# Dilated attention with queries and keys put in class order, a ones column in V, copies on GpSimd and loads queued between the quads

## The chip, the cores and the metric

The kernel runs on one core of a Trainium2 chip. The metric is the device time of one execution in microseconds (us), from runs on the chip; the kernel before takes 2574.51 us (median of 3 runs, 2571.3 to 2576.02). One further execution was profiled. TensorE is called PE, VectorE DVE, ScalarE ACT and GpSimd POOL; SP is the engine whose queue issues the DMAs.

## The reference, cut to what matters

Two transformer blocks follow each other over 1024 tokens of width 1024, in fp32. The change is inside the attention of the second block (8 heads of width 64), which mixes three dilated windows. Each branch is a softmax over keys at a distance that is a multiple of its dilation, and the branches are joined by their softmax denominators:

```python
DILATED_BRANCHES = ((128, 1), (512, 4), (2048, 16))

def dilated_window_branch(q, k, v, rel_bias, window, dil):
    half = window // (2 * dil)          # query p attends to keys p + dil*j, |j| <= half
    ...
    s = jnp.einsum('brnqhd,brnkhd->brnhqk', qb, kw).astype(jnp.float32)
    s = s + bias.transpose(2, 0, 1)
    s = jnp.where(valid[:, None], s, NEG_INF)
    m = jnp.max(s, axis=-1, keepdims=True)
    p = jnp.exp(s - m)
    den = jnp.sum(p, axis=-1, keepdims=True)
    o = jnp.einsum('brnhqk,brnkhd->brnqhd', (p / den).astype(v.dtype), vw)
    lse = (m + jnp.log(den))[..., 0].transpose(0, 1, 2, 4, 3)
    ...
    return o, lse

def dilated_attention(q, k, v, rel_bias):
    outs, lses = [], []
    for window, dil in DILATED_BRANCHES:
        o, l = dilated_window_branch(q, k, v, rel_bias, window, dil)
        outs.append(o)
        lses.append(l)
    w = jax.nn.softmax(jnp.stack(lses, axis=0), axis=0)
    return jnp.einsum('ibsh,ibshd->bshd', w.astype(q.dtype), jnp.stack(outs, axis=0))
```

The mixture of softmaxes is one softmax over all the keys of the three branches, a key counted once for each branch that has it.

## The kernel before, in words

Nearly all of the time is matmuls of weights against activations, each as three products of split operands (a high and a low part). The dilated attention stands between the projection of q and k (`d_run("qk", ...)`, line 1564) and the output projection (`wp_group`), at about 1684 to 1860 us of the span.

It is cut into quads: one quad (`dil_quad`, line 1805) is 128 queries of four heads. Branches 4 and 16 only join positions of one residue modulo 4, so they are done together as *class quads*: class c holds the 256 positions c, c+4, c+8, ..., and its bias carries log 2 where both branches have a key. There are 16 of them: `u` (which four heads) by `qb` (first or second 128 queries of the class) by `c`. The branch of dilation 1 is done in 16 *band quads*: 128 queries in a row, against 256 keys in a row (192 at the two ends).

The steps of a quad are a Python generator; `pump` (line 232) starts one new quad and lets each older one make a step, the youngest first, so the steps of several quads are interleaved in program order on every engine, and each engine runs its own order without overtaking. The steps: (1) `scores` (line 1254) makes eight PE matmuls, four with the 128-row operands and four with the 64-row low parts; DVE adds the bias and finds the row's extreme (L1831); ACT takes the exponential and sums it (L1834). (2) PE transposes the probabilities (L1842), ACT and DVE copy them out (L1845, L1847). (3) PE multiplies with V (L1861) and DVE copies the result (L1863). A class quad then writes its rows, the extremes and the sums to a DRAM buffer `cls_d` (L1865). A band quad loads the class rows of its own queries (tile `xc`, L1822, issued in its first step), and merges both with small DVE operations (L1870 to L1876) and POOL multiplications (L1877 to L1881); (4) two more PE transposes (L1887) put the result in the layout of the output projection (L1889, L1890).

Queries (`query_operand`, tiles `qst`) and keys (`key_operand`, tiles `kst`) are stored in token order. A class quad therefore reads both with a step of four elements (`qc`, `kc` in `scores`). V is loaded from DRAM: `vc` by class, four DMAs of 512 KB; `vb` for the bands, nine DMAs of up to 256 KB (L1575), all of them ahead of the first class quad on SP. The bias comes by `bias_load` (tiles `cb` for classes, `bb` for bands).

Tiles named `S` share 43 slots of 4 KB; a new tile waits until its slot's last reader is done. The row buffer `co` of a class quad comes from a ring of six. DMAs take turns on eight semaphores, so each waits for the one eight places ahead of it on SP.

Some of the split of the next weights runs on POOL while the band quads run (`self.low = nc.gpsimd`, L281).

Of the kernel before, what the change touches and what calls it, by code (L numbers as in the profile page):

```python
# [175 lines left out]
class Kern:  # L176
# [1062 lines left out]
    def key_operand(self):  # L1239

        nc = self.nc
        k = [self.S("kst", dt=F32R) for _ in range(3)]
        def put(h, ps):
            sl = slice(512 * h, 512 * h + 512)
            for s in range(2):
                pr = slice(64 * s, 64 * s + 64)
                nc.scalar.copy(k[s][pr, sl], ps[pr, :])
            for s in range(2):
                pr, po = slice(64 * s, 64 * s + 64), slice(64 - 64 * s, 128 - 64 * s)
                nc.vector.tensor_tensor(k[2][pr, sl], ps[pr, :], k[s][pr, sl].bitcast(F32), ALU.subtract)  # L1250
                nc.scalar.copy(k[s][po, sl], ps[pr, :])
        return k, put

    def scores(self, sc, qs, ks, q0, k0, step, nk):


        nc = self.nc
        qc = slice(q0 % 512, q0 % 512 + step * (P - 1) + 1, step)
        kc = slice(k0, k0 + step * (nk - 1) + 1, step)
        th = q0 // 512  # L1260
        for j in range(2):
            for s in range(2):
                nc.tensor.matmul(sc[s][:, 256 * j : 256 * j + nk], qs[j][th][:, s, qc], ks[j][s][:, kc],
                                 start=(j == 0), stop=False, skip_group_check=True)
        for j in range(2):
            for s in range(2):
                pr = slice(64 * s, 64 * s + 64)
                nc.tensor.matmul(sc[s][:, 256 * j : 256 * j + nk], qs[j][th][pr, s, qc], ks[j][2][pr, kc],
                                 start=False, stop=(j == 1), skip_group_check=True)


    def att1_quad(self, n, u, aq, ak, av, att):
# [6 lines left out]
        self.scores(sc, aq[2 * u : 2 * u + 2], [ak, ak], n * P, k0, 1, nk)  # L1279
# [168 lines left out]
    def block2(self, Z, x2_d):  # L1448
# [75 lines left out]
        def vc_load(c):  # L1524
            t = self.S("vc", [P, 2, 512])
            nc.sync.dma_start(t, vsrc[c].rearrange("(b p) c -> p b c", p=P))
            vc.append(t)

        vc, cb = [], []
        cls_d = dp.tile([SEQ, 2, 264], F32, name="cls_d")  # L1530
        qs, ks, kput = [None] * 4, [None] * 4, [None] * 4
        qput = [None] * 4
        cls = [self.dil_quad("c", (c, qb), u, qs, ks, vc, cb, cls_d)
# [3 lines left out]
        def qk_evac(p, s, ps):  # L1537
# [8 lines left out]
            if ch == 0:  # L1546
                if p == 1:
                    qs[s], qput[s] = self.query_operand()
                qput[s](th, src)
            else:  # L1550
                if p == 3:
                    ks[s], kput[s] = self.key_operand()
                kput[s](th, src)
            if p == 7 and s == 0:
                vc_load(0)
                cb.extend(self.bias_load(0, 384, "cb", range(4)))
            if p == 4 and s == 0:
                for c in range(1, 4):
                    vc_load(c)
# [7 lines left out]
        cb += self.bias_load(0, 384, "cb", range(4, 8))  # L1567
# [4 lines left out]
        vb = [self.S("vb", [P, 2, 512]) for _ in range(5)]  # L1572
        for m in range(9):
            lo, hi = max(0, P * m - 64), min(SEQ, P * m + 64)
            nc.sync.dma_start(vb[m // 2][0 : hi - lo, m % 2, :], v_d[lo:hi, :])  # L1575
        bb = self.bias_load(L_CLS, 256, "bb")
        while self.pend:
            self.pump()
# [14 lines left out]

        lead = 13
        gpo = self.bcast("gpo", a["g_post_mix_2"][0])
        self.low = nc.gpsimd
        wl = None
        for u in range(2):
            for n in range(NT):
                self.pend.append(self.dil_quad("b", n, u, qs, ks, vb, bb, cls_d, MX))  # L1600
                self.pump()
                i = NT * u + n
# [202 lines left out]
    def dil_quad(self, kind, where, u, qs, ks, vt, bias, cls_d, MX=None):  # L1805

        nc = self.nc
        if kind == "c":
            c, qb = where
            q0, k0, step, nk, b0 = c + 512 * qb, c, 4, 256, 128 - 128 * qb  # L1810
            segs = [(0, P, vt[c][:, 0, :]), (P, P, vt[c][:, 1, :])]
            co = self.H("co", [P, 264])
        else:
            n = where
            lo, hi = max(0, P * n - 64), min(SEQ, P * n + 192)
            q0, k0, step, nk, b0 = n * P, lo, 1, hi - lo, lo - (P * n - 64)
            segs = []
            for m in (n, n + 1):
                a0, a1 = max(0, P * m - 64), min(SEQ, P * m + 64)
                segs.append((a0 - lo, a1 - a0, vt[m // 2][0 : a1 - a0, m % 2, :]))  # L1820
            x2 = self.S("xc", [P, 2, 264])
            nc.sync.dma_start(x2[:, 0, :], cls_d[n * P : n * P + P, u, :])  # L1822
            co = x2[:, 1, :]
        sc = [self.PS("sc") for _ in range(2)]
        self.scores(sc, qs[2 * u : 2 * u + 2], ks[2 * u : 2 * u + 2], q0, k0, step, nk)
        z = self.S("z", [P, 4, 256])
        for s in range(2):
            for j in range(2):
                h, x = 4 * u + 2 * j + s, 2 * j + s
                nmc = co[:, 256 + x : 257 + x]  # L1830
                nc.vector.tensor_tensor_reduce(  # L1831
                    out=z[:, x, :nk], in0=sc[s][:, 256 * j : 256 * j + nk], in1=bias[h][:, b0 : b0 + nk], scale=-0.125,
                    scalar=BIG, op0=ALU.add, op1=ALU.min, accum_out=nmc)
                nc.scalar.activation(z[:, x, :nk], z[:, x, :nk], AF.Exp, bias=nmc, scale=-1.0,  # L1834
                                     accum_out=co[:, 260 + x : 261 + x])
        yield
        pT = self.S("pT", [P, 8, P])
        for g in range(2):
# [4 lines left out]
            if kind == "c" or segs[0][1] == segs[1][1]:  # L1843
# [14 lines left out]
        for x in range(4):  # L1858
            h = 4 * u + x
# [64 lines left out]
```

## Time and profile before

| | |
|---|---|
| runs, median (lowest to highest) | 2574.51 us (2571.3 to 2576.02) |
| profiled execution, its own time | 2574.72 us |
| its span | 2572.9 us |
| PE busy | 2504.7 us (97%) |
| DVE, ACT, POOL busy | 1765.6, 1142.2, 178.7 us |
| mean granted TensorE clock | 0.988 |

The span runs from the first to the last instruction; the profiled execution's own time is 1.8 us longer and 0.2 us above the median. PE is counted busy from a matmul's start to its modelled end, and the matmuls are pipelined, so a 97% busy PE may still hold short gaps. What a stage costs is read from the chain of waits, which gives each stretch of time to the instruction that held the end up.

### The profile page before, as it was taken

The page shows a single profiled execution, that of the slowest core. Times are in us where ns is not written, and L with a number is a line of the kernel's source. Part 1 is how long each engine was busy: PE and PEld are TensorE (multiplying, and loading weights), DVE is VectorE, ACT ScalarE, POOL GpSimd, SP SyncE. Part 2 cuts the span into 40 slices and gives each one's busy share as a digit, 9 for nine tenths or more (in the row PEclk, how much of TensorE's full clock was granted, in tenths as well). Part 3 has the DMA queues.
Part 4 walks back from the last instruction along what each step waited for, and adds up shares of the span by engine and source line. Part 5 has one row for each costly group of instructions (what it writes and reads, how often), then busy time and mean ns, then how long its engine had stood idle before and what let it go on. Part 6 is the DMA issues. An engine that isn't in the chain of part 4 may idle for free.

```text
span 2572.9 us, 31324 instructions
## 1 busy us (share of the span) xinstructions
PE 2504.7 (97%) x11857; PEld 2073.0 (81%) x11857; DVE 1765.6 (69%) x2789; ACT 1142.2 (44%) x2068; POOL 178.7 (7%) x236
## 2 busy tenths in 40 slices
PE   7999999999999999999999999999999999899998
PEld 5888888888787888878788777888887888788886
DVE  7664456556899755555799986666558444478888
ACT  5444445412425433333333644566436555553334
POOL 1000000000002000000000300002421000000006
PEclk9999999999999999999999999999899999999999
DMA  4333333135343122233433415221242333522334
GB/s 157 104 110 103 123 103 107 39 113 185 109 186 131 66 70 87 87 130 98 174 121 131 144 49 172 102 81 51 81 160 82 104 117 103 180 108 81 115 123 147
DMA packets 178703, 291.57 MB, mean 113 GB/s; under 512 B 10168, under 2 KB 84552, under 8 KB 178552
## 3 DMA queue, kind: packets, MB, share of 16 engines
q1 hardware_dynamic: 178552, 289.57, 33.1%
q8 instruction: 93, 1.52, 0.2%
q14 instruction: 58, 0.48, 0.1%
HBM read 212.89 MB, written 80.31 MB: 114 GB/s over the span
## 4 chain that ended last, share of the span: by engine, by line
PE 78%; DVE 13%; DMA 3%; ACT 3%; issue 2%; POOL 1%; SPq 0%; DVEq 0%; ACTq 0%; POOLq 0%
PE da L1201 6%; PE a L500 6%; PE a L502 6%; PE a L501 6%; PE da L1200 6%; PE da L1199 6%; PE db L1201 3%; PE db L1200 3%; PE db L1199 3%; PE b L502 3%; PE b L501 3%; PE b L500 3%; DVE wl L281 3%; PE pv L1861 2%; DVE midl L281 2%
## 5 line engine op out<-in xcount | busy, mean ns | idle before, releaser
L500 PE MATMUL a<-midh,ws 128*128 128x512 f32 x708 | 276.8, 391 | 9.1 <-DVE f L1669 8.0
L502 PE MATMUL a<-midh,ws 128*128 128x512 f32 x708 | 276.4, 390 | 0.0
L501 PE MATMUL a<-midl,ws 128*128 128x512 f32 x708 | 276.4, 390 | 0.0
L1201 PE MATMUL da<-wh,midl 128*128 128x512 f32 x624 | 245.1, 393 | 6.6 <-DVE midl L281 6.6
L1200 PE MATMUL da<-wl,midh 128*128 128x512 f32 x624 | 244.6, 392 | 3.4 <-DVE wl L281 3.4
L1199 PE MATMUL da<-wh,midh 128*128 128x512 f32 x624 | 246.0, 394 | 0.6 <-ACT midh L279 0.6
L279 ACT CAST midh<-mt 128x1024 fp32r<-128x1024 f32 x80 | 82.9, 1036 | 244.6 <-DVE mt L1142 81.3
L1201 PE MATMUL db<-wh,midl 128*128 128x512 f32 x436 | 171.0, 392 | 3.5 <-DVE midl L281 3.5
L1200 PE MATMUL db<-wl,midh 128*128 128x512 f32 x436 | 170.8, 392 | 2.2 <-DVE wl L281 2.2
L1199 PE MATMUL db<-wh,midh 128*128 128x512 f32 x436 | 171.1, 392 | 1.4 <-ACT midh L279 1.4
L500 PEld LDWEIGHTS a<-midh,ws 128*128 128x128 f32 x708 | 133.4, 188 | 38.7 <-issue 8.9
L501 PEld LDWEIGHTS a<-midl,ws 128*128 128x128 f32 x708 | 133.5, 189 | 27.7
L502 PEld LDWEIGHTS a<-midh,ws 128*128 128x128 f32 x708 | 133.5, 189 | 27.7
L279 ACT CAST ws<-tc 128x512 fp32r<-128x512 f32 x180 | 111.4, 619 | 88.3 <-DVE tc L414 87.1
L1201 PEld LDWEIGHTS da<-wh,midl 128*128 128x128 f32 x624 | 117.8, 189 | 34.5 <-DVE midl L281 10.3
L1200 PEld LDWEIGHTS da<-wl,midh 128*128 128x128 f32 x624 | 117.9, 189 | 29.0 <-DVE wl L281 4.8
L500 PE MATMUL b<-midh,ws 128*128 128x512 f32 x360 | 140.1, 389 | 0.0
L501 PE MATMUL b<-midl,ws 128*128 128x512 f32 x360 | 140.1, 389 | 0.0
L502 PE MATMUL b<-midh,ws 128*128 128x512 f32 x360 | 140.0, 389 | 0.0
L279 ACT CAST wh<-raw 128x1024 fp32r<-128x1024 f32 x121 | 120.6, 1037 | 42.0 <-DMA raw<-in_w_ff_dram 15.2
L1199 PEld LDWEIGHTS da<-wh,midh 128*128 128x128 f32 x624 | 118.0, 189 | 26.0 <-issue 1.2
L281 DVE TENSOR_TENSOR wl<-raw,wh 128x1024 fp32r<-128x1024 f32 x117 | 136.2, 1197 | 3.6 <-ACT wh L279 3.5
(348 smaller groups left out, 5822.8 us busy)
## 6 DMA issues: line engine op xcount, KB each, us to landing
raw<-in_w_ff_dram SPq DMA_DIRECT2D x31, 1024.0 KB, 5.4
mid_d<-f SPq DMA_DIRECT2D x108, 256.0 KB, 2.1
midr<-mid_d SPq DMA_DIRECT2D x52, 512.0 KB, 6.9
raw<-in_w_in_dram SPq DMA_DIRECT2D x22, 1024.0 KB, 5.4
x<-x_d SPq DMA_DIRECT2D x24, 512.0 KB, 4.5
raw<-in_w_up_dram SPq DMA_DIRECT2D x11, 1024.0 KB, 5.6
raw<-in_w_gate_dram SPq DMA_DIRECT2D x10, 1024.0 KB, 5.5
xt<-in_x_dram SPq DMA_DIRECT2D x16, 512.0 KB, 10.9
```

What stands on the lines that cost most here:

```text
L279: self.nc.scalar.copy(hi, s)
L281: e.tensor_tensor(lo, s, hi.bitcast(F32), ALU.subtract)
L500: nc.tensor.matmul(ps, hi[:, i], xh, start=(first and i == 0), stop=False, skip_group_check=True)
L501: nc.tensor.matmul(ps, hi[:, i], xl, start=False, stop=False, skip_group_check=True)
L502: nc.tensor.matmul(ps, lo[:, i], xh, start=False, stop=(i == 3), skip_group_check=True)
L1199: nc.tensor.matmul(ps, xh, wh, start=(kt == 0 and p in (1, 5, 2)), stop=False, skip_group_check=True)
L1200: nc.tensor.matmul(ps, xh, wl, start=False, stop=False, skip_group_check=True)
L1201: nc.tensor.matmul(ps, xl, wh, start=False, stop=(kt == m - 1), skip_group_check=True)
L1861: nc.tensor.matmul(pv[:, 64 * x : 64 * x + 64], pT[0:w, 2 * x + e, :], vv[:, 64 * h : 64 * h + 64], start=(e == 0), stop=(e == 1))
```

## The change

In words, part by part:

- Keys are stored class after class (`key_operand(4)`): the ACT and DVE operations that write them read their source with a step of four.
- Queries get a second copy in class order (`q_class`, tiles `qc`): 16 copies of 128x512, four of them on ACT and 12 on POOL. Class quads read `qc` and the keys without a step; band quads read `qst` and 256 keys in runs of 32. The four band quads at the ends make 16 score matmuls in place of 8.
- V tiles have 65 columns per head, the 65th filled with ones by POOL, so the product with V also gives the sum of the exponentials. ACT no longer sums (L1834's accumulate goes). V for the bands is loaded class by class, by heads: 36 DMAs of 32 rows (or 16) by four runs of 256 B for each `u`, 72 in place of nine. The classes' V is 16 DMAs in place of four.
- A band quad starts its extreme from that of its class rows, so these must have landed before its first DVE step; they are loaded one quad ahead (`c_load`). The merge becomes one POOL multiplication of the class rows, one DVE addition, a reciprocal and one POOL multiplication. Band quads get an empty step after the first.
- A class quad's result is copied out of PSUM by ACT, no longer by DVE.
- The loads move on SP: biases for heads 4 to 7, V for `u = 1`, V for the bands and their biases now stand between the class quads, V for the second half of the bands after band quad 4. POOL puts the band biases into class order (8 copies of 128x256).

The diff, cut to its core:

```diff
-    def key_operand(self):
+    def key_operand(self, r=1):
...
+            w = 512 // r
+            v = [x.rearrange("p (r j) -> p r j", r=r)[:, :, w * h : w * h + w] for x in k]
+            ps = ps.rearrange("p (j r) -> p r j", r=r)
             for s in range(2):
                 pr = slice(64 * s, 64 * s + 64)
-                nc.scalar.copy(k[s][pr, sl], ps[pr, :])
+                nc.scalar.copy(v[s][pr], ps[pr])
...
-    def scores(self, sc, qs, ks, q0, k0, step, nk):
+    def scores(self, sc, qs, ks, q, keys):
...
-                nc.tensor.matmul(sc[s][:, 256 * j : 256 * j + nk], qs[j][th][:, s, qc], ks[j][s][:, kc],
-                                 start=(j == 0), stop=False, skip_group_check=True)
+                for i, (o, n, f) in enumerate(keys):
+                    nc.tensor.matmul(sc[s][:, 256 * j + o : 256 * j + o + n], q(qs[j])[:, s], f(ks[j][s]),
+                                     start=(j == i == 0), stop=False, skip_group_check=True)
...
+        def v_slot(name, vs, u, i):
+            if i % 3 == 0:
+                t = self.S(name, [P, 3, 260])
+                nc.gpsimd.memset(t.rearrange("p s (h d) -> p (s h) d", d=65)[:, :, 64:65], 1.0)
...
+        def vb_load(u, m):
+            lo, hi = max(0, 32 * m - 16), min(256, 32 * m + 16)
+            v, w = v_slot("vb", vb, u, m), hi - lo
+            for c in range(4):
+                nc.sync.dma_start(
+                    v[c * w : c * w + w], vsrc[c, lo:hi, 256 * u : 256 * u + 256].rearrange("p (h d) -> p h d", d=64))
+
+        def q_class(s, th, copy):
+            yield
+            qc[s][th] = t = self.S("qc", [P, 2, 512], F32R)
+            for i in range(2):
+                copy(t[:, i, :].rearrange("p (r j) -> p r j", r=4), qs[s][th][:, i, :].rearrange("p (j r) -> p r j", r=4))
...
+            if step in (2, 3):
+                self.pend.extendleft(q_class(x, step - 2, nc.gpsimd.tensor_copy) for x in (2, 3))
+                self.pump(2)
+            if step == 4:
+                cb += self.bias_load(0, 384, "cb", range(4, 8))
+            if step == 5:
+                for i in range(8):
+                    vc_load(1, i)
+            if step == 11:
+                for m in range(9):
+                    vb_load(0, m)
+            if step in (11, 12):
+                h = 4 * (step - 11)
+                b, t = self.bias_load(L_CLS, 256, "bn", range(h, h + 4)), self.S("bb", [P, 4, 256])
+                for i in range(4):
+                    nc.gpsimd.tensor_copy(t[:, i, :].rearrange("p (g r j) -> p g r j", g=2, r=4),
+                                          b[i].rearrange("p (g j r) -> p g r j", g=2, r=4))
...
+        wl, nxt = None, c_load(0)
...
+                i = NT * u + n
+                x2, nxt = nxt, c_load(i + 1) if i < 15 else None
+                self.pend.append(self.dil_quad("b", n, u, qs, ks, vb, bb, x2, MX))
                 self.pump()
+                if i == 4:
+                    for m in range(9):
+                        vb_load(1, m)
...
+                least = BIG if kind == "c" else x2[:, 0, 260 + x : 261 + x]
+                for o, w, fb, fz in parts:
+                    nc.vector.tensor_tensor_reduce(
+                        out=fz(z[:, x, o : o + w]), in0=fz(sc[s][:, 256 * j + o : 256 * j + o + w]), in1=fb(bias[h]),
+                        scale=-0.125, scalar=least, op0=ALU.add, op1=ALU.min, accum_out=nm)
+                    least = nm
+                nc.scalar.activation(z[:, x, :nk], z[:, x, :nk], AF.Exp, bias=nm, scale=-1.0)
+        if kind == "b":
+            d = self.M("d", 4)
+            nc.gpsimd.tensor_tensor(d, co[:, 260:264], x2[:, 0, 260:264], ALU.subtract)
+            nc.scalar.activation(d, d, AF.Exp)
+            v = x2[:, 0, 0:260].rearrange("p (h d) -> p h d", d=65)
+            nc.gpsimd.tensor_tensor(v, v, d[:, :, None].to_broadcast([P, 4, 65]), ALU.mult)
+            yield
         yield
...
-        nc.vector.tensor_tensor(mn, x2[:, 0, 256:260], x2[:, 1, 256:260], ALU.min)
-        nc.vector.tensor_tensor(d, mn[:, None, :].to_broadcast([P, 2, 4]), x2[:, :, 256:260], ALU.subtract)
-        nc.scalar.activation(e, d, AF.Exp)
-        yield
-        nc.vector.tensor_tensor(d, e, x2[:, :, 260:264], ALU.mult)
-        nc.vector.tensor_tensor(rc, d[:, 0, :], d[:, 1, :], ALU.add)
-        nc.vector.reciprocal(rc, rc)
...
+        nc.vector.tensor_tensor(co[:, 0:260], pv[:, 0:260], x2[:, 0, 0:260], ALU.add)
+        sums = co[:, 0:260].rearrange("p (h d) -> p h d", d=65)
+        rc = self.M("rc", 4)
+        nc.vector.reciprocal(rc, sums[:, :, 64])
+        y = x2[:, 0, 0:256]
+        nc.gpsimd.tensor_tensor(y.rearrange("p (h d) -> p h d", d=64), sums[:, :, 0:64],
+                                rc[:, :, None].to_broadcast([P, 4, 64]), ALU.mult)
```

Three places show how the order moves. The first is SP's queue around the V of the bands, where `vb` is that V, `bn`/`bb` the band biases, `cls_d` the class quads' rows and `co` the row buffer of one class quad. Before:

```order
L1444 DMA cb_13182<-bias_d_8839 128x2x384
L1575 DMA vb_13184<-v_d 64x512
L1575 DMA vb_13184<-v_d 128x512
L1575 DMA vb_13185<-v_d 128x512 x2
L1575 DMA vb_13186<-v_d 128x512 x2
L1575 DMA vb_13187<-v_d 128x512 x2
L1575 DMA vb_13188<-v_d 64x512
L1444 DMA bb_13198<-bias_d_8839 128x4x256
L1444 DMA bb_13200<-bias_d_8839 128x4x256
L1865 DMA cls_d<-co_13160 128x264
L1865 DMA cls_d<-co_13202 128x264
```

With the change, the same engine at the rows of class quads 8 (`co_13525`), 9 (`co_13569`) and 10 (`co_13613`):

```order
L1940 DMA cls_d<-co_13525 128x264
L1548 DMA vb_13657<-v_d 16x4x64 x4
L1548 DMA vb_13657<-v_d 32x4x64 x8
L1548 DMA vb_13671<-v_d 32x4x64 x12
L1548 DMA vb_13685<-v_d 32x4x64 x8
L1548 DMA vb_13685<-v_d 16x4x64 x4
L1449 DMA bn_13699<-bias_d_8839 128x4x256
L1940 DMA cls_d<-co_13569 128x264
L1449 DMA bn_13750<-bias_d_8839 128x4x256
L1940 DMA cls_d<-co_13613 128x264
```

The nine loads stood ahead of every class quad's write; 36 now stand between the writes of quads 8 and 9.

The second place is SP's queue during the band quads, from the write of the last class quad (`co_13889`) on; `xc` are the class rows for band quads 3, 4, 5, 6 and 7:

```order
L1940 DMA cls_d<-co_13889 128x264
L1643 DMA xc_14035<-cls_d 128x264
L1643 DMA xc_14075<-cls_d 128x264
L1643 DMA xc_14126<-cls_d 128x264
L1548 DMA vb_14177<-v_d 16x4x64 x4
L1548 DMA vb_14177<-v_d 32x4x64 x8
L1548 DMA vb_14191<-v_d 32x4x64 x12
L1548 DMA vb_14205<-v_d 32x4x64 x8
L1548 DMA vb_14205<-v_d 16x4x64 x4
L1643 DMA xc_14219<-cls_d 128x264
L1643 DMA xc_14280<-cls_d 128x264
```

In the kernel before, only the 16 loads of class rows and a few others stand here. Now 36 more lie between the class rows for band quad 5 and those for band quad 6.

The third place is DVE's order in the second half of the bands, from the copy of the transposed probabilities of one quad to the start of the next. Before:

```order
L1847 COPY pT_14551<-tp_14558 128x512
L1863 COPY xc_14410<-pv_14564 128x256
L1870 TENSOR_TENSOR mn_14576<-xc_14410 128x4
L1871 TENSOR_TENSOR d_2639_14574<-mn_14576,xc_14410 128x8
L1874 TENSOR_TENSOR d_2623_14510<-d_2624_14511,xc_14352 128x8
L1875 TENSOR_TENSOR rc_14513<-d_2623_14510 128x4
L1876 RECIPROCAL rc_14513<-rc_14513 128x4
L1890 TENSOR_TENSOR mxl_1_2614_14463<-tq_14594,mxh_1_2613_14462 128x2x128
```

With the change:

```order
L1923 COPY pT_14650<-tp_14657 128x512
L1942 TENSOR_TENSOR xc_14336<-pv_14663,xc_14336 128x260
L1945 RECIPROCAL rc_14673<-xc_14336 128x4
L1956 TENSOR_TENSOR mxl_1_2599_14514<-tq_14682,mxh_1_2598_14513 128x2x128
L1899 ISA z_14699,xc_14572<-sc_14689,bb_13752,xc_14572 128x256
```

Four small operations with two SBUF operands are gone from DVE, and the row's extreme (L1899) now reads the class rows `xc`.

## Rows read from the trace of the kernel before

**Rows 1.** Windows: stretch in us, length, busy time of each engine (instructions), clock, DMA.
```profile
1640.00:1684.00 44.00, 44.00 (x195) 36.28 (x193) 27.08 (x35) 30.99 (x50) 0.00 (x0) 1.00 0.57 190
1704.00:1724.00 20.00, 20.00 (x144) 18.23 (x144) 11.04 (x45) 11.65 (x44) 0.00 (x0) 1.00 0.08 28
...
1795.00:1807.00 12.00, 10.73 (x61) 8.38 (x60) 11.54 (x38) 7.46 (x27) 9.87 (x13) 0.85 0.20 65
1807.00:1814.00 7.00, 7.00 (x34) 6.55 (x34) 5.14 (x19) 6.39 (x22) 3.62 (x4) 0.50 0.47 172
```

**Rows 2.** Chain of waits, one class quad: start us, us, engine and line.
```profile
1738.06 1.09 PE sc L1263 x4
1739.15 0.77 PE sc L1268 x4
1739.92 1.03 PE tp L1842 x8
1740.95 1.73 PE pv L1861 x16
```

**Rows 3.** Chain of waits, one band quad, and two transposes of a later one.
```profile
1777.76 0.53 PE sc L1263 x4
1778.28 0.43 PE sc L1268 x4
1778.72 1.02 PE tp L1842 x8
1779.74 1.73 PE pv L1861 x16
...
1785.19 0.23 PE tq L1887 x2
```

**Rows 4.** Groups of instructions on PE, 1786.2 to 1826.5 us: count, busy, mean ns.
```profile
L1861 PE MATMUL pv<-vb,pT 128*128 128x64 f32 (+1 forms) x128 | 19.1, 297 | 0.0
```

**Rows 5.** Timeline of DVE in the band quads: start us, us, instruction.
```profile
1789.56 0.17 DVE L1871 TENSOR_TENSOR d<-mn,xc 128x8 f32<-128x8 f32 x1
...
1792.68 2.27 DVE L1871 TENSOR_TENSOR d<-mn,xc 128x8 f32<-128x8 f32 x1
...
1799.35 0.42 DVE L1831 CUSTOM_DVE_ANT_0 z<-sc,bb 128x256 f32<-128x256 f32 x1
...
1799.69 0.42 DVE L1831 CUSTOM_DVE_ANT_0 z<-sc,bb 128x256 f32<-128x256 f32 x1
...
1803.36 2.26 DVE L1875 TENSOR_TENSOR rc<-d 128x4 f32<-128x4 f32 x1
```

**Rows 6.** Timeline of POOL in the same stretch.
```profile
1792.58 2.35 POOL L281 TENSOR_TENSOR wl<-raw,wh 128x1024 fp32r<-128x1024 f32 x1
...
1800.93 4.67 POOL L281 TENSOR_TENSOR wl<-raw,wh 128x1024 fp32r<-128x1024 f32 x2
```

**Rows 7.** DMA issues on SP by line: ns min/median/max of the issue, first and last start.
```profile
L1575 SPq DMA_DIRECT2D vb<-v_d x9: 320/430/577, 1673.8 to 1678.0; - x9
...
L1346 SPq DMA_DIRECT2D rvh<-rv_d x8: 359/371/2951, 486.6 to 568.6; - x8
...
L1420 SPq DMA_DIRECT2D oh<-in_c_onehot_dram x1: 415/415/415, 1103.2 to 1103.2; - x1
...
L299 SPq DMA_DIRECT2D raw<-in_w_att_o_dram x4: 595/609/734, 511.3 to 556.6; - x4
```

**Rows 8.** DMA issues by tile: count, KB each, median us from issue to landing.
```profile
cls_d<-co SPq DMA_DIRECT2D x16, 132.0 KB, 1.7
xc<-cls_d SPq DMA_DIRECT2D x16, 132.0 KB, 3.6
...
cb<-bias_d SPq DMA_DIRECT2D x4, 384.0 KB, 3.8
```

**Rows 9.** Groups, 1500 to 2100 us: ACT's exponentials of the bands, its writes of keys.
```profile
L1834 ACT ACTIVATE z<-z,xc 128x256 f32<-128x256 f32 (+1 forms) x64 | 30.9, 484 | 17.3 <-DVE xc L1831 16.2 <-issue 1.1
...
L1247 ACT CAST kst<-f 64x512 fp32r<-64x512 f32 x16 | 9.9, 618 | 6.2 <-DVE f L1545 6.0
```

More of the change, by code (lines that the diff above doesn't have):

```diff
@@ L1278, in att1_quad @@
         sc = [self.PS("sc") for _ in range(2)]
-        self.scores(sc, aq[2 * u : 2 * u + 2], [ak, ak], n * P, k0, 1, nk)
+        qo = n * P % 512
+        self.scores(sc, aq[2 * u : 2 * u + 2], [ak, ak], lambda t: t[n * P // 512][:, :, qo : qo + P],
+                    [(0, nk, lambda t: t[:, k0 : k0 + nk])])
         z = self.S("z", [P, 4, 256])
@@ L1571, in block2 @@
         MX.expect(("s", t) for t in range(NT))
[L1572 to L1576, printed above, removed]
-        while self.pend:
+        bb, step = [], 0
+        while self.pend:
+            step += 1
+            if step in (2, 3):
[15 more added lines that the diff above has]
+                                          b[i].rearrange("p (g j r) -> p g r j", g=2, r=4))
+                    bb.append(t[:, i, :])
             self.pump()
@@ L1802, in sgu_in, with dil_quad @@
         MX.missing -= {("s", 4 * half + t) for t in range(4)}
-    def dil_quad(self, kind, where, u, qs, ks, vt, bias, cls_d, MX=None):
+    def dil_quad(self, kind, where, u, qs, ks, vt, bias, rows, MX=None):
         nc = self.nc
@@ L1809, in dil_quad @@
             c, qb = where
-            q0, k0, step, nk, b0 = c + 512 * qb, c, 4, 256, 128 - 128 * qb
-            segs = [(0, P, vt[c][:, 0, :]), (P, P, vt[c][:, 1, :])]
+            q = lambda t: t[qb][:, :, P * c : P * c + P]
+            keys = [(0, 256, lambda t: t[:, 256 * c : 256 * c + 256])]
+            segs = [(e * P, P, vt[u, 2 * c + e]) for e in range(2)]
+            parts = [(0, 256, lambda b: b[:, 128 - 128 * qb : 384 - 128 * qb], lambda z: z)]
             co = self.H("co", [P, 264])
         else:
[L1814 to L1822, printed above, removed]
-            co = x2[:, 1, :]
+            n, x2 = where, rows
+            co = x2[:, 1, :]
+            q0 = P * (n % 4)
+            q = lambda t: t[n // 4][:, :, q0 : q0 + P]
+            k0, cut, k1 = max(0, 32 * n - 16), 32 * n + 16, min(256, 32 * n + 48)
+            segs = [(0, 4 * (cut - k0), vt[u, n]), (4 * (cut - k0), 4 * (k1 - cut), vt[u, n + 1])]
+            by_class = lambda t: t.rearrange("p (r j) -> p r j", r=4)
+            if k1 - k0 == 64:
+                keys = [(0, 256, lambda t: by_class(t)[:, :, k0:k1].rearrange("p r (g j) -> p g r j", g=2))]
+                parts = [(0, 256, lambda b: b, lambda t: t)]
+            else:
+                keys = [(o, w, lambda t, lo=k0 + o // 4, w=w: by_class(t)[:, :, lo : lo + w // 4]) for o, w, _ in segs]
+                parts = [(o, w, lambda b, e=e, at=(k0 + o // 4 + 16 - 32 * n) % 32, w=w:
+                          by_class(b[:, P * e : P * e + P])[:, :, at : at + w // 4], by_class)
+                         for e, (o, w, _) in enumerate(segs)]
         sc = [self.PS("sc") for _ in range(2)]
-        self.scores(sc, qs[2 * u : 2 * u + 2], ks[2 * u : 2 * u + 2], q0, k0, step, nk)
+        self.scores(sc, qs[2 * u : 2 * u + 2], ks[2 * u : 2 * u + 2], q, keys)
         z = self.S("z", [P, 4, 256])
+        nk = sum(w for _, w, _ in segs)
         for s in range(2):
```

82 lines of the change are left out of this document (36 added, 46 removed).

## The prediction

> **What bounds the kernel now.** I read the windows first, for the stretch that the change touches. In the class quads PE is never idle at the full clock, with DVE and ACT a little over half busy; in the band quads PE idles for 1.3 us of 12, DVE is busy 11.5 of 12, and the clock falls to 0.50 for 7 us behind that idle time [rows 1]. So the class quads are bound by PE, and the later band quads by something on DVE's side. The chain of waits then gives the price of a quad. A class quad is 1.09 + 0.77 us of scores, 1.03 of transposes and 1.73 of products with V: 4.62 us [rows 2]. A band quad that nothing disturbs is 0.53 + 0.43 + 1.02 + 1.73 = 3.71, and 3.94 with the 0.23 of its last two transposes [rows 3]. Both make eight score matmuls of 256 columns; only the class quad reads them with a step of four elements. Last I read DVE's timeline where the bands are slow: an operation on 128x8 that takes 0.17 us undisturbed takes 2.27, from the moment at which POOL has begun a 2.35 us subtraction until that ends, and again 2.26 under the next [rows 5, 6]. DVE's step on the scores, whose one operand comes from PSUM, isn't stretched.
>
> **Class quads: the step goes.** Scores in class order have the shape that the bands show undisturbed, so 1.86 us become 0.96: 0.90 saved in each of 16 quads, 14.4 us. All else that PE does there stays (65 columns instead of 64; 1.73 us for 16 instructions is 108 ns each, and a 65th column is nothing beside that). DVE and ACT spend 2.6 and 2.7 us per quad (11.04 and 11.65 over 20 us at 4.62); at 3.7 us per quad both still fit, the more since the copy of PV only changes from DVE to ACT and the reading of ACT's sum goes. What could take the gain back is a wait; those are counted below. I take 14.
>
> **Band quads: the stalls on DVE go.** From 1786.2 to 1826.5 us PE has 128 instructions of the product with V [rows 4], which at 16 a quad is 8 quads. Eight quads at 3.94 us are 31.5 of 40.3 us: 8.8 lost. The two stretched operations in rows 5 hold 2.1 us each too long, and the half-speed stretch behind them loses 3.5 (7 us at 0.50). The change leaves DVE no operation with two SBUF tensors in a band quad, only the addition (PSUM and SBUF), a reciprocal and what it had from PSUM. I take 8 of the 8.8; if the reciprocal is stretched by POOL as the others were, 5. The split of weights stays on POOL, and POOL's own work per quad falls from three wide operations to two. Keys in runs of 32 are taken as fast as keys in a row; were they as slow as keys at a step of four, 16 × 0.90 = 14 us would be lost here, which I hold unlikely since each run is read without a step. The four end quads make eight more short score matmuls each, at most 0.4 us a quad by the 0.05 to 0.13 us that score matmuls take: 1 us, inside what I left of the 8.8.
>
> **ACT and POOL: copies that are hidden.** ACT's four query copies at 0.62 us [rows 9] come when the first half of q is ready, a projection product and more before the quads, in a stretch where PE sets the pace: nothing. POOL's 12 copies have no row; half of the 2.35 us of a 1024-column operation [rows 6] is 1.2 each, 14 us, from about 1675 on. Class quads 4 to 7 need the first four (5 us, due 15 us after quad 0) and quads 8 on the rest (due after 30): hidden with room for twice the price. The keys are the open part: ACT writes them with 32 casts in all while it is busy 30.99 of 44 us [rows 1], and their reads now have a step of four. On PE that step took 273 ns for 256 columns, 1.07 ns a column; a cast of 512 takes 618 ns, 1.2 ns a column with its overhead, so the step may be free. If it adds 0.13 us each, 4 us on ACT, that fits. If it doubles a cast, 20 us do not fit, and some 8 of them would reach PE.
>
> The Trainium skill, SBUF — State Buffer, section "Door 1: The DMA port swizzle", says that accesses which each cross into a new 16-byte line pay a penalty, and that four fp32 elements is where it begins. For PE the trace agrees (1.09 against 0.53 us). For ACT no run here shows it; by the rule the sum would lose up to the 8 us just named.
>
> **SP: 36 loads in a row, twice.** This is the price of the change. An issue takes 0.32 us at the least, 0.36 with three dimensions, 0.415 for one over 32 partitions, 0.6 for one over 64 with three dimensions [rows 7]. The new loads have 32 partitions and three dimensions: I take 0.415 + 0.04, and 0.05 for the semaphore step between them (nine issues of median 0.43 took 4.7 us): 0.50 each, 18 us for 36. The bounds are 0.37 (13 us) and 0.65 to 0.70 (25 us); a packet or landing that holds the eight semaphores back leads to the upper end too.
>
> First wait. The rows of class quad 9 leave behind these loads; their buffer, one of six, is wanted again by quad 15. Take the end of quad 8's product with V as zero. The write of quad 9 lands after D for the loads, 0.7 for two writes, 0.4 for the bias load, and 1.7 to 3.6 of landing behind that [rows 8]: D + 3.7. Quad 15's first DVE step is due four steps and its scores later, 4 × 3.7 + 0.95 = 15.75, and PE feels it some 1.8 us after that, since DVE's four steps stand 0.34 apart [rows 5] and the last exponential takes 0.5 [rows 9], 1.9 of the 3.7 us until the transposes. The wait is D − 13.8: 4.2 us.
>
> Second wait. A band quad's first DVE step now reads the class rows. Those for band quad 0 are loaded behind the write of quad 13, which leaves at the end of the step before: 1.1 us for three issues, 3.6 to land, against 0.95 + 1.7 of slack: 2 us.
>
> Third wait. The second 36 loads need two slots, free after quads 14 and 15, so they start 1.9 us after band quad 1's step. The rows for band quad 6 then land at D + 4.8; they are due four steps of 3.94 and 0.95 later, at 16.7, and the slack is 2: D − 14, 4 us. Behind it stand the first DVE steps of all later quads.
>
> Each idle time costs clock: after 1.3 us of it the trace shows 7 us at 0.50 [rows 1], 3.5 lost. The short waits here may cost that or nothing; 4 us for the three. Together 4.2 + 2 + 4 + 4 = 14.2.
>
> The Trainium skill, DMA: Bandwidth & Descriptors, "Specifications", asks for at least 512 B per transfer for line rate; the new loads of V move 256 B pieces. No run here has such loads. If they landed so slowly that eight in flight held SP to the upper bound, it would be the slow rival's time.
>
> **Sum.** 2574.7 (the profiled execution's own time, 0.2 above the median) − 14 − 8 + 14.2 = 2566.9; I say 2566.5.
>
> **Rivals.** *The waits hide* (issues at the lower bound): D = 13.3, first and third waits are nothing, the second stays with 1 us of clock: 2574.7 − 14 − 8.8 + 3 = 2555. For it: median issues of 0.32 to 0.38 for most shapes in rows 7. Against: the one 32-partition issue. *The queue decides* (slower): at 0.70 an issue, D = 25; 11.2 + 2 + 11 of waits and 7 of clock are 31 against 22 gained: 2584. It decides from an issue of about 0.61 on (0.61 × 36 = 22: 8.2 + 2 + 8 + 6 = 24). For it: the 64-partition issues. Against: the wide 2-dimensional ones, and that no row shows a dependence on partitions alone. *The keys' casts double on ACT*: −14 − 8 + 14 + 8, 2575, no change. *The step is not why class scores are slow*, and the 14 us don't come: about 2580; the two kinds of scores differ in nothing else that PE sees, so I give it little.
>
> **Chances.** My forecast 0.45, the hidden waits 0.20, the queue 0.17, casts or another thing that cancels 0.15, the step 0.03. About 0.2% (5.1 us) is what a measurement of this kernel can tell from no change. The forecast's own range, issues of 0.43 to 0.56 (D of 15.5 to 20), is 2561 to 2571; its upper end touches no change, so of its 0.45 I count 0.07 there. Faster 0.38 + 0.20 = 0.58, same 0.07 + 0.13 = 0.20 with the rest, slower 0.22. The range, to the hidden waits on one side and to the queue on the other: 2552 to 2583.
>
> **What would show it.** Right: class quads at 3.7 us in the chain with scores of 0.53 and 0.43; no DVE operation of 2 us beside POOL's splits; two blocks of 36 issues on SP, 18 us each; DVE's first step of class quad 15 and of band quads 0 and 6 released by a DMA, with low clock behind them. Wrong in size: blocks of 13 or 25 us. Wrong in kind: class scores still at 1.8 us, ACT in front of PE at the end of the q and k projection, band scores slower than 0.96, or band quads waiting for POOL's copies of the bias, which come in behind the first block. The prediction falls if PE waits nowhere for `xc` or `co`, or if it waits there for more than 25 us.

## The result, and the profile after

The changed kernel takes 2590.29 us (median of 4 runs, 2588.52 to 2591.47) against 2574.77 for the kernel before beside it: a ratio of 1.0063 (95% interval 1.005 to 1.0076), slower by 15.5 us. Forecast were 2566.5, and 2552 to 2583 as the range.

The page's first section gives the totals of the changed kernel.

```profile
span 2586.7 us, 31402 instructions
...
PE 2498.1 (97%) x11889; PEld 2067.5 (80%) x11889; DVE 1756.5 (68%) x2741; ACT 1156.4 (45%) x1960; POOL 186.7 (7%) x252
```

PE is busy for 6.6 us less (2504.7 before), though the class scores alone save more than that, and the span is 13.8 us longer. What PE does at a low clock counts as busy for longer, so the time was lost in waiting and in clock. To place it I take three milestones of PE from the answers on its tiles: the first score of the classes, the last product with V of the classes (`vc`), the last matmul of the output projection (`wp`). The kernel before (count, ns min/median/max, first and last start):

```profile
L1263 PE MATMUL sc<-kst,qst x128: 249/418/599, 1683.7 to 1842.0; 128*128 128x256 f32 x112, 128*128 128x192 f32 x16
...
L1861 PE MATMUL pv<-vc,pT x256: 222/275/276, 1694.6 to 1763.6; 128*128 128x64 f32 x128
...
L603 PE MATMUL wp<-wh,mxl x128: 389/389/628, 1827.0 to 1931.7; 128*128 128x512 f32 x128
```

The changed kernel:

```profile
L1265 PE MATMUL sc<-kst,qc x64: 276/280/580, 1694.0 to 1751.9; 128*128 128x256 f32 x64
...
L1936 PE MATMUL pv<-vc,pT x256: 222/275/476, 1703.6 to 1775.3; 128*128 128x65 f32 x128
...
L603 PE MATMUL wp<-wh,mxl x128: 388/389/398, 1837.0 to 1945.5; 128*128 128x512 f32 x128
```

The quads start 10.3 us later. The class leg (start of the first score to start of the last product) takes 81.3 us instead of 79.9, the band leg (from there to the start of the last `wp`) 170.2 instead of 168.1. Behind it both spans have 641.2 us left. 10.3 + 1.4 + 2.1 = 13.8: all of the difference.

The chain of waits shows what did come as forecast, a class quad and a late band quad:

```profile
1736.78 0.53 PE sc L1265 x4
1737.30 0.43 PE sc L1271 x4
1737.74 1.02 PE tp L1918 x8
1738.76 1.73 PE pv L1936 x16
...
1832.76 0.53 PE sc L1265 x4
1833.29 0.43 PE sc L1271 x4
1833.73 1.03 PE tp L1918 x8
1834.75 1.74 PE pv L1936 x16
```

3.71 us a class quad against 4.62 [rows 2]; the scores take 0.96 instead of 1.86, 0.90 less, 14.4 over 16 quads. Keys in runs of 32 cost the bands nothing (0.53 and 0.43 again). By this estimate the class leg would be 79.9 − 14.4 = 65.5 us if PE waited and ran slow no more than before, and 15.8 of its 81.3 are new waits and clock.

The windows of the changed kernel (columns as in [rows 1]) show where PE idles and at what clock it runs:

```profile
1640.00:1684.00 44.00, 39.05 (x165) 31.45 (x164) 24.93 (x27) 34.38 (x35) 0.36 (x3) 0.96 0.32 90
...
1749.90:1762.30 12.40, 7.92 (x69) 7.04 (x67) 2.86 (x15) 3.80 (x11) 2.52 (x5) 0.87 0.57 161
1762.30:1772.00 9.70, 6.51 (x30) 5.59 (x29) 4.29 (x23) 3.50 (x11) 3.02 (x6) 0.50 0.33 96
1772.00:1776.00 4.00, 3.98 (x18) 3.98 (x19) 0.85 (x6) 1.93 (x6) 0.82 (x2) 0.50 0.27 72
1776.00:1799.70 23.70, 19.98 (x151) 17.56 (x149) 12.58 (x49) 10.76 (x29) 5.28 (x14) 0.93 0.35 88
1799.70:1813.20 13.50, 13.50 (x83) 13.23 (x84) 7.81 (x32) 6.99 (x17) 5.76 (x8) 0.62 0.17 56
1813.20:1836.70 23.50, 23.50 (x171) 20.65 (x172) 18.00 (x76) 18.14 (x45) 18.11 (x21) 0.93 0.36 122
```

In the q and k projection PE, never idle before, now misses 5 us of 44 while ACT is busy 34 instead of 31. Later three idle times stand out (4.5, 3.2 and 3.7 us, 11.4 together). Behind the first PE runs at a granted 0.50, the lower level of 1.2 GHz; behind the third the mean of 13.5 us is 0.62. The clock lost, busy time times what is missing from 1.00, is 1.0 + 3.3 + 2.0 + 1.4 + 5.1 + 1.6 = 14.4 us over the last six rows.

DVE's timeline names what ended the long waits (in brackets: idle time before, and its releaser):

```profile
1760.19 0.42 DVE L1899 CUSTOM_DVE_ANT_0 z<-sc,cb 128x256 f32<-128x256 f32 x1 [9.00 <-DMA cls_d<-co]
...
1768.15 0.28 DVE L1899 CUSTOM_DVE_ANT_1 z<-sc,bb,xc 128x64 f32<-128x64 f32 x1 [5.26 <-DMA xc<-cls_d]
...
1798.72 0.48 DVE L1899 CUSTOM_DVE_ANT_0 z<-sc,bb,xc 128x256 f32<-128x256 f32 x1 [5.88 <-DMA xc<-cls_d]
```

These are the three that were forecast: class quad 15 waits for its row buffer, band quads 0 and 6 for their class rows. SP's timeline has the two blocks that stand ahead of the first and the third:

```profile
1737.59 17.99 SPq L1548 DMA_DIRECT2D vb<-v_d  x36
...
1778.01 18.28 SPq L1548 DMA_DIRECT2D vb<-v_d  x36
```

18.0 and 18.3 us, as forecast (18). The answer for this line gives one issue and its landing:

```profile
L1548 SPq DMA_DIRECT2D vb<-v_d x72: 365/430/1436, 1737.6 to 1795.9; - x72
...
DMA to landing us min/median/max: 1.7/1.9/2.9
```

0.43 us an issue and, in the chain of waits, 0.04 to the next; with a few longer issues 0.50 on the mean of the block. The loads land 2.9 us after issue at the latest, and eight issues take 3.8, so it was not slow landing that held SP. The Trainium skill, DMA: Bandwidth & Descriptors, "Specifications", asks for at least 512 B per transfer for line rate. The pieces of 256 B did not set the time here, the number of issues did: in run e2 below, with pieces of 256 B again and a quarter of the issues, the block takes 5.2 us.

ACT's writes of the keys, the part that I had left open:

```profile
L1250 ACT CAST kst<-f x16: 1085/1096/1113, 1652.0 to 1688.0; 64x512 fp32r<-64x512 f32 x16
L1254 ACT CAST kst<-f x16: 1083/1097/1131, 1654.3 to 1690.2; 64x512 fp32r<-64x512 f32 x16
```

1.10 us against 0.62 [rows 9]. From 1677.9 to 1691.3 us the chain of waits runs through these casts one behind the other. Behind them come the last writes of the queries, 7.0 us as before (6.9), and the first class scores stand on the chain at 1698.30 (1687.91 in that of the kernel before):

```profile
1689.13 1.08 ACT kst L1254
...
1690.23 1.08 ACT kst L1254
1691.31 0.48 ACT qst L1233
```

### The profile page after: what moved, and what is told of

It is laid out like the page before. It is cut to its first block, busy times and chain, and to the rows that moved or that the text cites. A ratio compares the mean times of both kernels' runs of the same rounds, so it can differ in the third digit from the quotient of the medians.

```text
span 2586.7 us, 31402 instructions
## 1 busy us (share of the span) xinstructions
PE 2498.1 (97%) x11889; PEld 2067.5 (80%) x11889; DVE 1756.5 (68%) x2741; ACT 1156.4 (45%) x1960; POOL 186.7 (7%) x252
## 4 chain that ended last, share of the span: by engine, by line
PE 71%; DVE 14%; DMA 6%; ACT 4%; issue 2%; SPq 1%; POOL 1%; DVEq 0%; ACTq 0%; POOLq 0%
PE a L500 6%; PE a L502 6%; PE a L501 6%; PE da L1201 5%; PE da L1200 5%; PE da L1199 5%; DVE wl L281 3%; PE b L500 3%; PE b L502 3%; PE b L501 3%; PE db L1201 3%; PE db L1200 3%; PE db L1199 3%; DVE midl L281 2%; PE pv L1936 2%
```

## The experiments

Two theories. *Casts*: ACT's 32 casts of the keys set the pace before the first quad (in its last 10 us, 1684 to 1694, ACT is busy 9.81 and DVE 5.99). *Queue*: the two blocks of 36 loads on SP make PE wait, and its clock falls behind that. The runs take each away alone and both together. The ratios are to the kernel before on the same chip (2573.3 to 2574.1 us). The changed kernel itself was timed only beside a kernel before of 2574.8 us, so "less than the changed kernel" can be off by the 0.7 to 1.5 us between these.

**e1_keys_once: the class order made once, by DVE.**

```diff
-            ps = ps.rearrange("p (j r) -> p r j", r=r)
+            ps = ps.rearrange("p (r j) -> p r j", r=r)
...
-                nc.vector.tensor_tensor(src, ps, self.part(p, s), ALU.add)
+                by = (lambda t: t) if ch == 0 else (lambda t: t.rearrange("p (j r) -> p r j", r=4))
+                nc.vector.tensor_tensor(src if ch == 0 else src.rearrange("p (r j) -> p r j", r=4),
+                                        by(ps), by(self.part(p, s)), ALU.add)
```

> The changed kernel (2590.3 us), but the class order of the keys is made once, by DVE in the addition that fills f (its two sources read with a step of four), so that ACT's 32 casts and DVE's 16 subtractions read in a row again. Theory casts: the 32 casts at 1.10 us instead of 0.62 make ACT the pace of the last 40 us of the q and k projection and move the first class quad from 1687.9 to 1698.3 us; they fall to 0.62, the first class quad starts 8 to 11 us earlier, and the time is 2580 (2578 to 2583). DVE's 16 additions may rise from 0.61 or 0.70 to about 1.06, as its subtractions did, 6 us on an engine that is busy 25 of 44 there. Theory queue: all that was lost is lost behind the two blocks of 36 loads, and an earlier start only lengthens the waits there: 2590 (within 2).

Measured: 2579.89 us (ratio 1.003, 1.0016 to 1.0044), 10.4 less than the changed kernel. The first class score is at 1684.2, the casts of this run:

```profile
L1250 ACT CAST kst<-f x16: 611/617/623, 1653.0 to 1679.6; 64x512 fp32r<-64x512 f32 x16
```

DVE's 16 subtractions are plain again too (0.69 us); its eight additions rose from 0.69 to 1.06 us and hid. The price of writing the keys is real and not covered by the waits behind it. (The nine runs spread from 2573.6 to 2590.3, with mean clocks between 0.980 and 0.988, so the 10.4 is not sharp.)

**e2_vb_blocks: 18 loads in place of 72.** `vb_d` holds V block by block.

```diff
                 nc.sync.dma_start(v_d[t * P : (t + 1) * P, :], f)
+                for e in range(2):
+                    m = t + e
+                    w = 16 if m in (0, 8) else 32
+                    o = 16 * (1 - e) if w == 32 else 0
+                    nc.sync.dma_start(
+                        vb_d[P * m : P * m + 4 * w].rearrange("(r j) c -> j r c", r=4)[o : o + 16], f[64 * e : 64 * e + 64])
...
-            for c in range(4):
-                nc.sync.dma_start(
-                    v[c * w : c * w + w], vsrc[c, lo:hi, 256 * u : 256 * u + 256].rearrange("p (h d) -> p h d", d=64))
+            nc.sync.dma_start(
+                v[0 : 4 * w], vb_d[P * m : P * m + 4 * w, 256 * u : 256 * u + 256].rearrange("p (h d) -> p h d", d=64))
```

> The changed kernel, but V for the bands is also written to DRAM block by block (16 more writes of 64x512 behind the projection of V), so that each band block of 128 rows is one load of 128x4x64 in place of four of 32x4x64: 18 loads in place of 72, in the same places. Packets stay at 256 B in the loads. Theory queue: a block on SP falls from 18 to about 4 us, DVE's first step of class quad 15 (9.0 us of waiting) and of band quad 6 (5.9 us) no longer wait for a DMA, and the low clock behind them goes: PE idled 11.4 us between 1744 and 1804 us and lost some 15 us of clock up to 1824, of which I expect 15 to 25 back: 2570 (2565 to 2576). Theory casts: the waits are only a part, the rest stays: 2580 or more. If the size of the packets and not the number of loads held the block, it stays near 18 us and nothing changes.

Measured: 2577.36 us (1.0013, 1.0004 to 1.0022), 12.9 less, under the 15 to 25 expected. SP's timeline of this run:

```profile
1740.48 5.21 SPq L1554 DMA_DIRECT2D vb<-vb_d  x9
...
1773.72 5.15 SPq L1554 DMA_DIRECT2D vb<-vb_d  x9
```

The first and third waits are gone, the second is not. The first class score comes at 1697.2, 3.2 us later than in the changed kernel. That the 16 more writes do this is not shown: in five runs whose kernels are the same up to there (e1, e6, e7, e9, e10) it comes between 1683.5 and 1687.2, so this milestone is good to some 4 us only.

**e3_both: e1 and e2 together.**

> Both edits: class order of the keys made once by DVE, and 18 band loads of V in place of 72. If the two causes are separate and both real, their gains add: 2590 - 10 - 20 = 2560 (2553 to 2567), faster than the kernel before (2574.8). If one hides the other, it is no better than the better of the two alone.

Measured: 2566.1 us (0.9972, 0.9962 to 0.9982), 24.2 less than the changed kernel; alone the two gave 10.4 and 12.9, 23.3. The causes are separate and add.

**e4_before_step: the kernel before, with the step in the writing of the keys alone.** The edit is `key_operand(4)` with the function of the changed kernel; it puts the step into ACT's 32 casts and DVE's 16 subtractions.

> The kernel before, with one part of the change alone: ACT and DVE write the keys in class order, reading with a step of four. Everything else is as before, so the scores are taken from keys in another order than they should be; only the time is of interest. Theory casts: the casts go from 0.62 to 1.10 us and the first class quad moves from 1687.9 to about 1698: 2584 (2581 to 2588). Theory queue: the quads' own slack takes it up, 2575 to 2578.

Measured: 2585.34 us (1.0047, 1.0035 to 1.0059), 12 slower, with the casts at 1.10 us. This one part, alone, turns the kernel before into a slower one by most of what the whole change lost.

**e5_xc_early: class rows two quads ahead.**

```diff
+            if step in (13, 14):
+                xcs.append(c_load(len(xcs)))
...
-                x2, nxt = nxt, c_load(i + 1) if i < 15 else None
+                if i < 14:
+                    xcs.append(c_load(i + 2))
+                x2 = xcs[i]
```

> The changed kernel (2590.3 us), but the class rows of the bands are loaded two quads ahead in place of one, those for band quads 0 and 1 before class quads 13 and 14 have run their steps; the two blocks of 36 loads stay. Theory waits: the second wait (band quad 0, DVE idle 5.3 us) goes; of the third (band quad 6, 5.9 us) about one quad's time goes, since now band quad 7's rows stand behind the block, due 3.9 us later; the first (class quad 15, 9.0 us) stays. PE gets back some 4 us of idle time and as much of clock: 2582 (2578 to 2586). Theory one price: the low clock behind the first wait covers the other two, and nothing comes back: 2588 to 2591.

Measured: 2586.79 us (1.0052, 1.004 to 1.0064), 3.5 less, between the two answers. It tells little. The first wait changed its place: DVE's copy of the transposed probabilities now waited for POOL's copy of the bias, which comes in behind the same block (I take it that the earlier `xc` tiles shift the slots; no run shows that):

```profile
1762.85 0.69 DVE L1927 COPY pT<-tp 128x512 f32<-128x512 f32 x1 [11.74 <-POOL bb L1627]
```

**e6_keys_spread: e1, and the 72 loads issued four per quad.**

```diff
-            if step == 11:
-                for m in range(9):
-                    vb_load(0, m)
+            if 6 <= step < 15:
+                vb_load(0, step - 6)
...
-                if i == 4:
-                    for m in range(9):
-                        vb_load(1, m)
+                if 4 <= i < 13:
+                    vb_load(1, i - 4)
```

> The changed kernel with the class order of the keys made once by DVE, and with the 72 loads of V kept as they are but issued four per quad, behind the class rows of the next quad, in place of two blocks of 36. Theory blocks: what counts is what queues behind 36 loads, not their number; the first and third waits go, and without the 16 more writes of the blocked V: 2563 (2558 to 2568). Theory number: SP still spends 0.48 us on each of 72 loads and the eight semaphores hold the loads behind them back, so waits come back in other places: 2572 to 2578.

Measured: 2562.06 us (0.9955, 0.9942 to 0.9968), 17.8 less than e1, and 12 faster than the kernel before. SP still issues 72 loads of 0.43 us; what counted was what queued behind 36 of them in a row. Its milestones:

```profile
L1265 PE MATMUL sc<-kst,qc x64: 276/280/553, 1685.1 to 1742.6; 128*128 128x256 f32 x64
...
L1936 PE MATMUL pv<-vc,pT x256: 222/275/477, 1694.7 to 1759.0; 128*128 128x65 f32 x128
...
L603 PE MATMUL wp<-wh,mxl x128: 388/390/398, 1810.8 to 1919.7; 128*128 128x512 f32 x128
```

The class leg is 73.9 us, the band leg 160.7: 7.4 less than before the change. Against the estimate of 65.5, 8.4 us are left in the class leg. DVE's and PE's timelines show the second wait in it:

```profile
1751.83 0.28 DVE L1899 CUSTOM_DVE_ANT_1 z<-sc,bb,xc 128x64 f32<-128x64 f32 x1 [6.32 <-DMA xc<-cls_d]
```

```profile
1755.70 3.68 PE L1936 MATMUL pv<-vc,pT 128*128 128x65 f32 x16 [4.41 <-ACT co L1939]
```

The product takes 3.68 us there instead of 1.73, at the lower clock. From 1750 to 1759 PE is busy 4.59 us at a mean granted 0.65: 4.4 us of idle time and 1.6 of clock, 6.0 of the 8.4.

**e7_keys_spread_xc: e6 with the class rows two quads ahead (the edit of e5).**

> The one before, with the class rows loaded two quads ahead, the first two before class quads 13 and 14. Theory waits: the second wait goes too (PE idled 3 to 4 us between the last class quads and the first bands and ran below full clock for some 10 us behind it): 2556 (2552 to 2561). If the wait is only in front of another one (POOL's copies of the band biases, the rows of the bias), it is as the run before.

Measured: 2562.24 us (0.9962, 0.9945 to 0.9979), no gain in the median, but 12 runs spread from 2554.4 (mean clock 0.992) to 2579.9 (0.982). In the profiled one (2578.3) DVE no longer waits for a load, and the class leg is 68.7 us, 5.2 less than in e6:

```profile
L1265 PE MATMUL sc<-kst,qc x64: 278/281/585, 1683.5 to 1741.5; 128*128 128x256 f32 x64
...
L1940 PE MATMUL pv<-vc,pT x256: 222/275/418, 1693.1 to 1752.2; 128*128 128x65 f32 x128
```

PE idles little, and yet it falls to the lower clock and stays there:

```profile
1744.00:1764.00 20.00, 19.57 (x142) 17.18 (x140) 12.38 (x56) 12.42 (x35) 4.09 (x10) 0.88 0.33 98
1764.00:1784.00 20.00, 20.00 (x99) 18.98 (x99) 7.77 (x28) 6.87 (x18) 4.15 (x9) 0.50 0.16 45
1784.00:1804.00 20.00, 20.00 (x98) 19.49 (x98) 9.54 (x45) 7.65 (x19) 5.43 (x9) 0.50 0.14 38
```

40 us at 0.50 with PE busy throughout, behind 20 us in which it idled 0.43. The load's wait can be removed; what the clock then does differs from execution to execution, and why stays open.

**e8_blocks_xc: e3 with the edit of e5.**

> Class order of the keys made once by DVE, 18 loads of blocked V in two blocks of nine, class rows two quads ahead. The first class quad started 3 to 5 us later where V was written twice. If the 16 more writes cost that, this is 3 to 5 us slower than four loads per quad with the same class rows: 2560 (2556 to 2565); if they are free, it is the same or faster.

Measured: 2563.03 us (0.9962, 0.9948 to 0.9976), 2557.2 to 2571.1. The spread hides the 3 to 5 us in question: inconclusive on the writes. The second wait is gone here too, and the class leg is 68.3 us (1687.5 to 1755.8).

**e9_first_spread and e10_second_spread: e1 with one half of e6's edit each.**

> The changed kernel with the class order of the keys made once by DVE (2579.9 us with both blocks, 2562.1 with both spread), and only the first block of 36 loads issued four per quad; the second block stays behind the rows of band quad 5. If the first block's price is the larger (the class stage, from the first scores to the last product with V, took 81.3 us with the blocks and 73.9 without), this gives 10 to 13 of the 17.8 us: 2568 (2565 to 2571). By the terms forecast for the waits (4.2 and 2 for the first and second, 4 for the third, clock 4) it would give about two thirds, 2568 as well; if the third wait and its clock are the larger part, 2574.

> The same with only the second block issued four per quad, the first block staying between the rows of class quads 8 and 9. If the two prices add, this gives the rest of the 17.8 us, 5 to 8: 2573 (2570 to 2576). If the low clock behind the first wait covers the third, it gives nothing, 2579 to 2580.

Measured: 2572.37 us (0.9996, 0.9986 to 1.0006) and 2570.21 (0.9985, 0.9976 to 0.9994): 7.5 us for the first block and 9.7 for the second, 17.2 of the 17.8 that both give. They add, and the second looks the dearer one, against my expectation; e1's and e9's runs spread over 17 and 15 us (e9: 2564.5 to 2579.8), so the 2 us between them are not certain. The legs of the two profiles place each price. e9, then e10:

```profile
L1265 PE MATMUL sc<-kst,qc x64: 278/280/580, 1687.2 to 1744.3; 128*128 128x256 f32 x64
...
L1937 PE MATMUL pv<-vc,pT x256: 222/275/477, 1696.4 to 1760.5; 128*128 128x65 f32 x128
...
L603 PE MATMUL wp<-wh,mxl x128: 388/389/400, 1820.9 to 1929.3; 128*128 128x512 f32 x128
```

```profile
L1265 PE MATMUL sc<-kst,qc x64: 277/280/552, 1685.9 to 1743.3; 128*128 128x256 f32 x64
...
L1937 PE MATMUL pv<-vc,pT x256: 222/275/477, 1695.4 to 1766.6; 128*128 128x65 f32 x128
...
L603 PE MATMUL wp<-wh,mxl x128: 389/389/402, 1818.3 to 1927.8; 128*128 128x512 f32 x128
```

With the first block spread the class leg is 73.3 us (e6 has 73.9) and the band leg 168.8; with the second spread they are 80.7 and 161.2 (e6: 160.7). So the first block costs 7 to 8 us, in the class leg, and the second 8 to 9, in the band leg.

**e11_dve_write and e12_act_write: the step on the writing side.** Both issue the loads as e6 does. e11 against e6:

```diff
-                by = (lambda t: t) if ch == 0 else (lambda t: t.rearrange("p (j r) -> p r j", r=4))
-                nc.vector.tensor_tensor(src if ch == 0 else src.rearrange("p (r j) -> p r j", r=4),
+                by = (lambda t: t) if ch == 0 else (lambda t: t.rearrange("p (j r) -> p j r", r=4))
+                nc.vector.tensor_tensor(src if ch == 0 else src.rearrange("p (r j) -> p j r", r=4),
```

> The fastest steady version so far (class order once by DVE, loads four per quad, 2562.1 us), but DVE's addition reads in a row and writes with a step of 128 elements instead of reading with a step of four and writing in a row. If any step past four elements costs DVE what the reading cost (1.06 us instead of 0.70 per 128x512), the time is the same; if only reading with a step costs, the additions are 0.70 and the time is the same or 1 us lower, since DVE is not the pace there.

e12 against the changed kernel, besides the loads:

```diff
-            v = [x.rearrange("p (r j) -> p r j", r=r)[:, :, w * h : w * h + w] for x in k]
-            ps = ps.rearrange("p (j r) -> p r j", r=r)
+            v = [x.rearrange("p (r j) -> p j r", r=r)[:, w * h : w * h + w, :] for x in k]
+            ps = ps.rearrange("p (j r) -> p j r", r=r)
```

> The changed kernel with the loads four per quad and the 32 casts still putting the keys in class order, but reading in a row and writing with a step of 256 elements. If the step costs ACT as much on the writing side (1.10 us), the first class quad starts as late as in the changed kernel and the time is 2572 (2570 to 2575); if writing with a step is free (0.62), it is 2562, as with the order made by DVE.

Measured: 2563.2 us (0.996, 0.9947 to 0.9974) and 2575.77 (1.0007, 0.9998 to 1.0015). DVE's additions that write with a step, and ACT's casts that do:

```profile
L1575 DVE TENSOR_TENSOR f<-da,yp 128x512 f32<-128x512 f32 x4 | 4.4, 1090 | 0.1
```

```profile
L1254 ACT CAST kst<-f x16: 1056/1152/1345, 1657.5 to 1694.8; 64x512 fp32r<-64x512 f32 x16
```

The step costs as much on either side. Against e6, with the same loads and plain casts, e12 is 13.7 us slower: the writing of the keys again.

## Why the prediction was wrong

Point by point, in time of the profiled executions.

*Class quads, −14: right.* 14.4 by the chain of waits in undisturbed quads. No run has a class leg of 65.5 us; the shortest are 68.3 and 68.7 (e8, e7), so up to 3 us of it did not show as time.

*Band quads, −8: right.* 7.4 in e6, whose blocks are spread. That this is the stalls on DVE is read from the timeline; no run takes them away alone. They are gone: in e6 POOL splits weights from 1785.22 to 1787.58, and DVE's operations inside that stretch take what they take elsewhere (0.43 and 0.18):

```profile
1786.54 0.43 DVE L1942 TENSOR_TENSOR xc<-pv,xc 128x260 f32<-128x260 f32 x1 [0.84 <-PE pv L1936]
1787.00 0.18 DVE L1945 RECIPROCAL rc<-xc 128x4 f32<-128x4 f32 x1
```

*ACT and POOL, nothing: wrong, and the first failed step.* "so the step may be free" was taken from PE's 1.07 ns a column; a cast with the step takes 1.10 us, not 0.62, and 10.3 us reached PE (12 in e4, 10.4 in e1). The forecast's own sign of it, ACT in front of PE at the end of the q and k projection, is in the chain above. I took a rate on one engine as evidence for another, though the nearest row, PE's own 1.09 us against 0.53, said that the step doubles. The rival that doubled the casts priced them at 8, but gave 2575 because it left the other terms alone. The Trainium skill, SBUF — State Buffer, "Door 1: The DMA port swizzle", says that accesses which each cross into a new 16-byte line pay a penalty. The traces agree for ACT and DVE too: 0.62 to 1.10 us, 0.69 to 1.06. POOL's and ACT's query copies did hide (1.16 and 1.12 us each, POOL's from 1693.2 to 1705.9), though ACT's had been taken at 0.62, again without the step.

*SP, the waits: the places right, the idle time right, the clock wrong.* Both blocks took 18 us. PE's idle times are 4.5, 3.2 and 3.7 us where 4.2, 2 and 4 stood: 11.4 against 10.2. But "4 us for the three" of clock was 14.4 (windows above). Each wait, with its clock: 7.4 for the first (15.8 in the class leg, less the 8.4 left in e6; e9 gives 7.5), at most 8.4 for the second, 9.5 for the third (2.1 + 7.4; e10 gives 9.7). Of the 8.4, 5.2 and 5.6 came back in the class legs of e7 and e8, where the second wait is gone, and nothing in e7's median; for the other 3 us no run has a cause. I had seen one stretch of 7 us at 0.50 behind 1.3 us of idle time [rows 1] and priced three such waits at little more than one of it. The second has no slack to speak of: in e6 DVE idles 6.32 us before it against some 1.6 in the quads before, 4.7 late, and PE idles 4.41, since ACT's copies for the last class quads stand behind the band's exponentials in its order, not ahead of them as my 1.7 us of slack supposed.

The sum as it was: −14.4 − 7.4 + 10.3 + 7.4 + 8.4 + 9.5 = 13.8, the difference of the spans. It closes by construction, since the waits are what the legs leave over; the check from outside is the windows, whose 11.4 us of idle time and 14.4 of clock make 25.8 against 25.3 for the three. Of the 21.6 us between 13.8 and the forecast's −7.8, casts are 10.3 and the waits with their clock 11.1.

## What to carry to other kernels

When a layout change takes a step out of one engine's reads, the step turns up in whoever writes the new layout: price it there from the nearest row with a step, on whatever engine (here the time rose by 1.5 to 2 times on PE, ACT and DVE), do it once, on the engine that has time, ahead of the operations that repeat. Small loads are priced by what queues behind them: the same 72 issues cost 17.8 us more in two blocks than with four between the quads. Short waits of PE cost more in clock here (14.4 us) than in idle time (11.4), so several of them should each be priced with their own stretch of low clock.

## What was not expected of the hardware

- A step of 256 or 128 elements on the writing side costs ACT and DVE what a step of four costs on the reading side: 1.11 to 1.15 us against 1.10 on ACT, 1.09 against 1.06 on DVE, from 0.62 and 0.69.
- PE stayed at a granted 0.50, the lower level of 1.2 GHz, for 40 us while busy (e7). Runs of that one kernel differ by 25 us, and their mean clocks go from 0.992 to 0.982; 0.010 of 2560 us is 26 us, so the clock can be all of the difference (an estimate).
- The DVE step on the scores takes 0.48 us with the starting extreme from a tile, as the bands now have it, and 0.42 with a constant, as the classes do and the bands did [rows 5]: 0.06 more. No run changes this alone.
